# Expert units in another order: units of four experts beside single ones, and TensorE's order written by hand

## The chip, the cores and the metric

One core of one Trainium2 chip runs the whole program. A time is the device time of one execution in microseconds (us). Of the kernel before there are three timed runs (median 2342.96 us) and one execution under the hardware profiler, from which all rows below come.

## The reference, cut to what matters

Two model blocks run one after the other on 512 tokens of width 1024. The change lies in the last stage alone, the mixture of experts of the second block. Each token picks 6 of 64 experts and a shared one, and each expert is

```
def swiglu(x, wg, wu, wd):
    return (jax.nn.silu(x @ wg) * (x @ wu)) @ wd
# wg, wu: 1024 x 256 and wd: 256 x 1024 per expert
routed = sum over the 6 chosen experts of  w[token, e] * swiglu(h[token], wg[e], wu[e], wd[e])
y      = x + g2 * (routed + swiglu(h, shared));   out = rms_norm(y, final_g)
```

All is float32. The weights of the 64 experts are 201 MB and must all be read from HBM, whatever the tokens choose.

## The kernel before

The experts are ranked by how many tokens chose them, and `self.units` cuts the ranking into units of 128 token slots: 2 units of two experts at 64 slots whose experts are known ahead (T), 16 units of one expert at 128 slots (S), 14 units of two at 64 (P), 4 units of four at 32 (Q). The shared expert makes 4 more units of 128 tokens (H). `ORDER` (L2318) lists them in batches of two units of one kind. The loop of `moe` (L2189) walks through the units. For unit n:

- `start(n + 2)` orders the weights of the unit after next on SP's queue: three pieces of 1 MB per expert (gate and up for the first half of the width, for the second half, down) in the ring `er` of nine buffers (`NER`). A load waits only for a free buffer, so SP runs ahead of TensorE by up to nine pieces. For the first unit of a batch it also builds the one-hot matrix of the slots, and `slots` (products `pt`) turns it into token numbers and weights.
- `split_gu` (units S and H): ScalarE rounds each 128x512 weight tile to fp32r (`eh`, L2012), VectorE forms the rest (`el`, L2016); eight buffers each (`NEH`). A product is then three fast fp32r matmuls, eh·xh, el·xh, eh·xl. Units P and Q multiply the raw fp32 tiles: each expert uses 64 or 32 columns of the array, and those of the unit's two or four experts run side by side if they follow each other.
- `gate_up` (products `pg`, L2067), then silu on ScalarE and the multiplication on VectorE (`sg`), `hidden` (two transposes `pht`), `down` (products `py`, L2110), and the multiplication by g2 into `y`.
- `gather` (products `px`, L2048): half of the token rows of the next batch, picked with its one-hot matrix; 32 matmuls of 256 columns for each unit. `px` has two PSUM banks.
- `scatter`: GpSimd adds the `y` of the unit before to the output rows in HBM.

What stands in the loop is not the order in which engines work: the scheduler of the tile layer orders each engine's queue by its own estimates. At run time each engine works through its queue in order. `first`, `batch_slots(b)` and `c0 = 128 * (u % 2)` assume that both units of a batch have equally many experts. `finish` adds everything up and normalizes.

```
    NER = 9
    NEH = 8
    ONES, PAIRS, FOURS = 16, 28, 16
    ORDER = "T0 Q0 S0 P0 S1 P1 S2 P2 S3 H0 Q1 H1 S4 P4 S5 P5 S6 P6 S7 P3"
```

Of the kernel before, what the change touches and what calls it, by code (L numbers as in the profile page):

```python
# [7 lines left out]
F32 = mybir.dt.float32  # L8
F32R = mybir.dt.float32r
# [3 lines left out]
ALU = mybir.AluOpType  # L13
AX = mybir.AxisListType
# [23 lines left out]
class Builder:  # L38
# [1832 lines left out]
    def overflow_list(self):  # L1871

        nc = self.nc
        M = self.mx
        cnt = self.eid[:, 1]
        thr = M.tile([128, 4, 64], F32, name="thr")
        for a, b, c in self.CAPS:
            nc.gpsimd.memset(thr[:, 0, a:b], float(c))
        for j in range(1, 4):
            nc.gpsimd.tensor_scalar(thr[:, j], thr[:, 0], 128.0 * j, None, op0=ALU.add)  # L1880
        fcv = self.big("ovf").rearrange("p (a b c) -> p a b c", a=4, b=4)
        f, c, v = (fcv[:, i] for i in range(3))
        fl = lambda t: t.rearrange("p r e -> p (r e)")
        nc.vector.tensor_tensor(f, cnt[:, None, :].to_broadcast([128, 4, 64]), thr, op=ALU.is_gt)
        nc.vector.memset(v, 1.0)
        nc.vector.tensor_tensor_scan(fl(c), fl(v), fl(f), 0.0, op0=ALU.mult, op1=ALU.add)
        self.novf = self.mo.tile([128, 1], I32, name="novf")
        nc.vector.tensor_copy(self.novf, c[:, 3, 63:64])
        nc.vector.tensor_mul(c, c, f)
        nc.vector.tensor_scalar(c, c, -1.0, None, op0=ALU.add)  # L1890
        col = M.tile([128, 3], F32, name="ovcol", bufs=1)
        d = self.big("ovd")[:, :384].rearrange("p (a b) -> p a b", a=3)
        bc = lambda t: t[:, None, :].to_broadcast([128, 4, 64])
        for i, src in enumerate((bc(self.eid[:, 0]), bc(self.slot[:, 0:64]), thr)):
            nc.vector.scalar_tensor_tensor(v, c, self.pcol, src, op0=ALU.is_equal, op1=ALU.mult, accum_out=col[:, i:i + 1])
            nc.vector.tensor_scalar(d[:, i], self.ident, col[:, i:i + 1], None, op0=ALU.mult)
        pd = self.psg.tile([128, 3, 128], F32, name="pd", tag="px", bufs=2)
        nc.tensor.matmul(pd, self.ones, d, start=True, stop=True)
        self.ovexp = self.mo.tile([128, 2, 128], I32, name="ovexp")
        nc.vector.tensor_copy(self.ovexp, pd[:, 0:2])  # L1900
        self.ovoff = self.mo.tile([128, 128], F32, name="ovoff")
        nc.vector.tensor_copy(self.ovoff, pd[:, 2])
# [29 lines left out]
            self.places(oh, num)  # L1932
            self.finish([(self.ysplit(job["y"]), oh)])

    def onehot(self, pos, n, w):

        oh = self.xp.tile([128, NT, 256], F32R, name="oh", tag="oh", bufs=2)
        shape = [128, NT, n, w]
        self.nc.vector.tensor_tensor(oh[:, :, :n * w].rearrange("p t (n w) -> p t n w", n=n),
                                     pos[:, :, :, None].to_broadcast(shape),  # L1940
                                     self.slot1[:, None, None, :w].to_broadcast(shape), op=ALU.is_equal)
        return oh
# [30 lines left out]
            nc.vector.reduce_sum(num, sv[:, :, :u, 0], axis=AX.X)  # L1973
            nc.vector.tensor_scalar(num, num, 1024.0, None, op0=ALU.add)

    def batch_slots(self, b, num=None):

        rs = self.units[2 * b] + self.units[2 * b + 1]
        n, r = len(rs), slice(rs[0], rs[-1] + 1)
        u = slice(2 * b, 2 * b + 2)  # L1980
        oh = self.oh[b] = self.onehot(self.pos[:, :, r], n, 256 // n)
        self.slots(oh, self.vals[:, :, r], n, 256 // n, self.idx[:, r], self.wt[:, u], num)

    def raw(self, pool=None):
        return (pool or self.er).tile([128, 2048], F32, name="er", tag="er")
# [43 lines left out]
                for dn, raw in zip(job["dn"], job["raw"]):  # L2029
                    dn.append(self.wsplit(raw[2][:, k, h * 512:h * 512 + 512]))  # L2030

    def rows(self, rhs, h, whole, to=None):


        nc = self.nc
        n = rhs[0][1].shape[-1]
        x = [self.xp.tile([128, 4, 256], F32 if whole else F32R, name="xh", tag="xh", bufs=3) if to is None else
             to.rearrange("p (k n) -> p k n", k=4)]
        if not whole:
            x.append(self.my.tile([128, 4, 256], F32R, name="xl", tag="xl", bufs=2))  # L2040
        for q in range(2):
            for i in range(len(x)):
                px = self.psg.tile([128, 2, 256], F32, name="px", tag="px", bufs=2)
                for f in range(2):
                    k = 4 * h + 2 * q + f
                    ops = [(self.xt[t][p], oh) for t, oh in rhs for p in ((0, 1) if whole else (i,))]
# [3 lines left out]
                dst = x[i][:, 2 * q:2 * q + 2, :n]  # L2050
                if i == 0:
                    nc.scalar.copy(dst, px[:, :, :n])
                else:
                    nc.vector.tensor_copy(dst, px[:, :, :n])
        return x

    def gate_up_half(self, job, h):
# [3 lines left out]
        whole = job["whole"]  # L2061
        for k in range(4 * h, 4 * h + 4):
            x = [x[:, k % 4] for x in job["xs"][h]]
            for i, (x, w) in enumerate(((x[0], None),) if whole else ((x[0], 0), (x[0], 1), (x[1], 0))):
# [62 lines left out]
    def moe(self):  # L2127
# [8 lines left out]
        jobs = {}  # L2136
        nu = len(self.units)
        n = self.NSTAT // 2
        first = dict(T=0, S=n // 2, P=(n + self.ONES) // 2, Q=(n + self.ONES + self.PAIRS // 2) // 2)
        order = []  # L2140
        for b in self.ORDER.split():
            n = int(b[1:])
            if b[0] == "H":
                order += [f"s{2 * n}", f"s{2 * n + 1}"]
            else:
                order += [2 * (first[b[0]] + n), 2 * (first[b[0]] + n) + 1]

        def start(n):

# [14 lines left out]
            b = u // 2  # L2164
            if n == len(order) - 2:
                self.num = self.mj.tile([128, 2], F32, name="num")
            if b not in self.oh:
                self.batch_slots(b, self.num if n == len(order) - 2 else None)
            w = 128 // len(rs)
            es = []  # L2170
            for r in rs:
# [8 lines left out]
            jobs[u] = dict(whole=whole, down=whole, wt=self.wt[:, u:u + 1], c0=128 * (u % 2), raw=raw,  # L2180
                           parts=[(w * j, w) for j in range(len(rs))], caps=slots)
        def gather(n, h):

            if n >= len(order):
                return
# [2 lines left out]
                t = int(u[1])  # L2188
                rhs = [(t, self.idr[:, 128:384]), (t + 1, self.idr[:, 0:256])]  # L2189
            else:  # L2190
                rhs = [(t, self.oh[u // 2][:, t]) for t in range(NT)]
            xs[n] = xs.get(n, []) + [self.rows(rhs, h, jobs[u]["whole"])]
        xs = self.xs
        start(0)
        start(1)
        for n, u in enumerate(order):
            j = jobs[u]
            start(n + 2)
            j["xs"] = xs[n - n % 2]
# [10 lines left out]
                self.last_begin()  # L2210
            if "mem" not in j:
                self.gate_up(j)
                self.hidden(j)
            gather(n - n % 2 + 2, n % 2)
            if not j["down"]:
                self.split_down(j)
            if n and not late:
                for i in range(1, 4):
                    self.scatter(jobs[order[n - 1]], i)
            if "mem" not in j:  # L2220
                self.down(j)
            if n == 8:
                self.overflow_list()
                self.last_gain()

        nc.vector.tensor_scalar(self.fst[:, 0], j["sg"][:, :NT], 0.0, 1.0, op0=ALU.mult, op1=ALU.add)
        nc.scalar.activation(self.fst[:, 1], self.fst[:, 0], AF.Abs_reciprocal_sqrt)
# [5 lines left out]
    def last_gain(self):  # L2233

        nc = self.nc
        r = self.big("fgr")[:KD, :128]
        nc.sync.dma_start(r, self.a["final_g_2"].rearrange("(k p) -> k p", p=128))
# [5 lines left out]
    def last_begin(self):  # L2243
# [4 lines left out]
        for h in range(2):  # L2248
# [2 lines left out]
                nc.tensor.matmul(p[:, k], self.fgc[:, 4 * h + k:4 * h + k + 1].to_broadcast([128, 128]), self.ident, start=True, stop=True)  # L2251
            nc.scalar.copy(self.fgb[:, 512 * h:512 * h + 512], p)
        self.sum = [r[:, i * D:(i + 1) * D] for r in (self.raw() for _ in range(NT // 2)) for i in range(2)]
        for t in range(NT):
            nc.sync.dma_start(self.sum[t], self.racc[self.nsc % 2][t * 128:(t + 1) * 128])
# [13 lines left out]
    def finish(self, ys, more=None):  # L2269
# [4 lines left out]
        rows = [slice(t * 128, t * 128 + 128) for t in range(NT)]  # L2274
        if more:
            for t in range(NT):
                nc.sync.dma_start(more[t], self.racc[1 - self.nsc % 2][rows[t]])
        po = {}

        def mm(t, h):  # L2280
# [132 lines left out]
```

## Time and profile before

| what | value |
|---|---|
| timed runs, three | 2337.82, 2342.96, 2346.70 us |
| profiled execution, its own time | 2337.98 us |
| its span | 2335.9 us |
| TensorE busy (page) | 2220.7 us, 95% |
| VectorE, ScalarE, GpSimd busy | 59%, 43%, 18% |
| the stage of the experts | from about 1690 us to the end |
| its last `py` product | begins at 2303.70 us |
| mean transfer rate over the span | 178 GB/s |

In the page's strip of 40 slices the DMA engines are busy to 2 to 5 tenths before the stage and to 8 or 9 tenths in it, with 316 to 385 GB/s. TensorE's granted clock (PEclk) is full through nearly all of it. Busy time of TensorE counts from the start of a matmul to its modelled end, and matmuls overlap, so the distance from one start to the next tells more.

### The profile page before, as it was taken

How to read it: one execution, taken by the hardware profiler on the slowest of the kernel's cores; microseconds unless marked ns; L12 is line 12 of the kernel's file. 1: busy time of each engine (PE TensorE's matmuls, PEld its weight loads, DVE VectorE, ACT ScalarE, POOL GpSimd, SP SyncE). 2: the span in 40 equal slices, each digit the busy share in tenths (PEclk: the TensorE clock that was granted, in tenths of full speed). 3: DMA queues.
4: the chain of work that ended last, by engine and by line, in shares of the span. 5: the costliest groups of instructions: out<-in, count | busy, mean ns of one | idle time of the engine just before them, and what ended most of it. 6: DMA issues, size and time to landing. Idle time of an engine off the chain costs nothing. (4 is left out here: it accounts for less than half of the span.)

```text
span 2335.9 us, 31811 instructions
## 1 busy us (share of the span) xinstructions
PE 2220.7 (95%) x11699; PEld 1668.9 (71%) x11699; DVE 1381.9 (59%) x2439; ACT 1015.4 (43%) x1743; POOL 427.2 (18%) x354
## 2 busy tenths in 40 slices
PE   8999999999999999999889969999999999999995
PEld 6888888888777888888767656776655666466662
DVE  3658837854887686487557785774424555144444
ACT  4445515534786454354455525542313334133332
POOL 3023203310000322122302530002022011111110
PEclk9999999999999999999999978999999999999998
DMA  4235535435222443435045533326399989889894
GB/s 158 100 128 178 167 102 183 130 104 143 59 62 64 146 137 123 137 124 160 23 127 143 150 76 92 87 71 235 145 349 385 356 316 325 326 320 340 322 341 172
DMA packets 243809, 414.97 MB, mean 178 GB/s; under 512 B 35030, under 2 KB 135732, under 8 KB 243652
## 3 DMA queue, kind: packets, MB, share of 16 engines
q1 hardware_dynamic: 233444, 393.87, 48.7%
q0 software_dynamic: 5184, 13.90, 3.1%
q10 hardware_dynamic: 5024, 5.15, 1.0%
q8 instruction: 93, 1.52, 0.3%
q14 instruction: 64, 0.52, 0.1%
HBM read 378.93 MB, written 40.22 MB: 179 GB/s over the span
## 5 line engine op out<-in xcount | busy, mean ns | idle before, releaser
L93 DVE TENSOR_TENSOR wlo<-wraw,whi 128x2048 fp32r<-128x2048 f32 (+3 forms) x83 | 182.5, 2199 | 206.0 <-ACT whi L92 205.7
L135 PE MATMUL mm<-sgh,whi 128*128 128x512 f32 x768 | 300.8, 392 | 0.9 <-DVE hT L204 0.9
L136 PE MATMUL mm<-sgl,whi 128*128 128x512 f32 x768 | 299.2, 390 | 0.0
L137 PE MATMUL mm<-sgh,wlo 128*128 128x512 f32 x768 | 297.5, 389 | 0.0
L92 ACT CAST whi<-wraw 128x2048 fp32r<-128x2048 f32 (+3 forms) x83 | 146.1, 1761 | 210.6 <-PE mm L136 160.1
L746 POOL TENSOR_TENSOR adaacc<-adaacc,adaw 128x512 f32<-128x512 f32 x84 | 146.3, 1741 | 434.8 <-ACT adaw L745 431.7
L2067 PE MATMUL pg<-er,xh 128*64 128x512 f32 (+1 forms) x768 | 181.1, 599 | 4.7 <-DMA er<-in_exp_w_up 4.6
L2123 POOL DMA_INDIRECT racc<-y,idx x60 | 91.6, 1526 | 509.3 <-DVE y L2113 464.4
L135 PEld LDWEIGHTS mm<-sgh,whi 128*128 128x128 f32 x768 | 144.2, 188 | 30.9 <-issue 1.5
L137 PEld LDWEIGHTS mm<-sgh,wlo 128*128 128x128 f32 x768 | 144.2, 188 | 30.3 <-issue 0.2
L136 PEld LDWEIGHTS mm<-sgl,whi 128*128 128x128 f32 x768 | 144.2, 188 | 29.8 <-issue 0.5
L135 PE MATMUL mm<-ach,whi 128*128 128x512 f32 (+1 forms) x374 | 141.3, 378 | 0.0
L137 PE MATMUL mm<-ach,wlo 128*128 128x512 f32 (+1 forms) x374 | 140.9, 377 | 0.0
L136 PE MATMUL mm<-acl,whi 128*128 128x512 f32 (+1 forms) x374 | 140.8, 377 | 0.0
L2016 DVE TENSOR_TENSOR el<-er,eh 128x512 fp32r<-128x512 f32 x200 | 129.5, 685 | 18.2 <-ACT eh L2012 16.6
L2012 ACT CAST eh<-er 128x512 fp32r<-128x512 f32 x200 | 115.4, 620 | 50.8 <-PE pg L2067 32.3
L907 PE MATMUL mm<-nmh,zhi 128*128 128x512 f32 (+2 forms) x264 | 106.7, 405 | 10.5 <-DVE k L877 5.8
L2113 DVE TENSOR_TENSOR y<-py,g2b 128x512 f32<-128x512 f32 x76 | 52.3, 689 | 102.6 <-PE py L2110 102.4
L2067 PEld LDWEIGHTS pg<-er,xh 128*64 128x64 f32 (+1 forms) x768 | 48.3, 127 | 90.4 <-issue 85.6
L908 PE MATMUL mm<-nml,zhi 128*128 128x512 f32 (+2 forms) x264 | 103.9, 394 | 1.4 <-DVE nml L809 1.4
L909 PE MATMUL mm<-nmh,zlo 128*128 128x512 f32 (+2 forms) x264 | 103.0, 391 | 1.8 <-DVE zlo L899 1.8
L427 ACT ACTIVATE cv<-a,convw 128x512 f32<-128x512 f32 x88 | 70.5, 811 | 74.0 <-DVE a L425 74.0
(687 smaller groups left out, 5123.3 us busy)
## 6 DMA issues: line engine op xcount, KB each, us to landing
er<-in_exp_w_gate SPq DMA_DIRECT2D x128, 512.0 KB
er<-in_exp_w_up SPq DMA_DIRECT2D x128, 512.0 KB
er<-in_exp_w_down SPq DMA_DIRECT2D x64, 1024.0 KB
wraw<-in_f_w_in SPq DMA_DIRECT2D x32, 1024.0 KB
adaw<-in_ada_w SPq DMA_DIRECT2D x96, 256.0 KB
wraw<-in_f_w_down SPq DMA_DIRECT2D x16, 1024.0 KB
zraw<-in_w_in SPq DMA_DIRECT2D x30, 512.0 KB
wraw<-in_a_w_in SPq DMA_DIRECT2D x8, 1024.0 KB
```

Of the source, the lines that this page charges most:

```text
L92: nc.scalar.copy(hi[:, :n], raw[:, :n])
L93: nc.vector.tensor_sub(lo[:, :n], raw[:, :n], hi[:, :n])
L135: nc.tensor.matmul(to, wh[:, cols], xh, start=first, stop=False)
L136: nc.tensor.matmul(to, wh[:, cols], xl, start=False, stop=False)
L137: nc.tensor.matmul(to, wl[:, cols], xh, start=False, stop=last)
L746: nc.gpsimd.tensor_add(acc, acc, t)
L907: nc.tensor.matmul(ps[:n, part], hi[:, k, :n], xh, start=first and k == ks[0], stop=False)
L908: nc.tensor.matmul(ps[:n, part], hi[:, k, :n], xl, start=False, stop=False)
L909: nc.tensor.matmul(ps[:n, part], lo[:, k, :n], xh, start=False, stop=last and k == ks[-1])
L2012: nc.scalar.copy(hi, r)
L2016: nc.vector.tensor_sub(lo, r, hi)
L2067: nc.tensor.matmul(job["pg"][b:b + n], x[:, c:c + n], job["raw"][j][h][:, k % 4] if whole else job["gu"][j][k][w], start=k == 0 and i == 0 ...
```

## The change

`ORDER` becomes a list of letters, one per unit, in pairs, and each letter takes the next unit of its kind; the last two letters take the first units of theirs. Each Q now shares a batch with an S, so that the four Q stand in four batches instead of two. A mixed batch needs rows of two sorts from one gather: `rows` writes the exact rows of the Q half (rounded part plus rest, added on VectorE) and the rounded part and rest of the S half separately, in halves of 128 columns; `mixed_slots` does the slots of both. `gather` is cut in two: its first quarter-product stands between `gate_up` and `hidden`, its second between `hidden` and `down`, and `slots` move behind `gate_up`. TensorE's queue keeps this order as written (`manual_schedule`). The overflow list's product and the load of the last gain move one or two units.

```diff
-    def batch_slots(self, b, num=None):
+    def batch_onehot(self, us):
+        ra, rb = (self.units[u] for u in us)
+        if len(ra) == len(rb):
+            return self.onehot(self.pos[:, :, ra[0]:rb[-1] + 1], 2 * len(ra), 128 // len(ra))
+        oh = None
+        for i, r in enumerate((ra, rb)):
+            oh = self.onehot(self.pos[:, :, r[0]:r[-1] + 1], len(r), 128 // len(r), oh, 128 * i)
+        return oh
+    def batch_slots(self, us, oh, num=None):
...
+            self.mixed_slots(us, oh)
...
-    def rows(self, rhs, h, whole, to=None):
+    def rows(self, rhs, h, whole, to=None, x=None, qs=(0, 1)):
...
+            if mixed:
+                xs = x.pop().rearrange("p k (i n) -> p i k n", i=2)
+                x = [x[0][:, :, :128], xs[:, 0], xs[:, 1]]
+        part, full = (slice(0, 128), slice(128, 256))[::1 if whole == "split first" else -1]
-        for q in range(2):
-            for i in range(len(x)):
+        for q in qs:
+            for i in range(2 if mixed else len(x)):
...
+                if mixed and i == 0:
+                    nc.scalar.copy(dst[0], px[:, :, full])
+                    nc.scalar.copy(dst[1], px[:, :, part])
+                elif mixed:
+                    nc.vector.tensor_add(dst[0], px[:, :, full], dst[0])
+                    nc.vector.tensor_copy(dst[2], px[:, :, part])
...
-        for n, u in enumerate(order):
+        def unit(n, u):
...
             if "mem" not in j:
                 self.gate_up(j)
+            if n % 2 == 0:
+                slots(n + 2)
+            gather(n - n % 2 + 2, n % 2, 0)
+            if "mem" not in j:
                 self.hidden(j)
-            gather(n - n % 2 + 2, n % 2)
+            gather(n - n % 2 + 2, n % 2, 1)
             if not j["down"]:
                 self.split_down(j)
...
+        with self.tc.manual_schedule(engines={mybir.EngineType.PE}):
+            for n, u in enumerate(order):
+                unit(n, u)
...
-    ORDER = "T0 Q0 S0 P0 S1 P1 S2 P2 S3 H0 Q1 H1 S4 P4 S5 P5 S6 P6 S7 P3"
+    ORDER = "TT SQ SS PP SS SS PP SQ SS SS PP SQ HH PP PP HH PP SQ SS PP"
```

SP's queue at the first unit behind the two T units, before: the expert's number is read, then gate and up of the first half (a piece is a gate and an up load into one `er` buffer, or a down load); then the next expert's.

```order
L2172 TENSOR_LOAD eidi
L2002 ISA
L2002 DMA er<-in_exp_w_gate 128x1024
L2002 ISA
L2002 DMA er<-in_exp_w_up 128x1024
L2172 TENSOR_LOAD eidi
```

The same place in the changed kernel.

```order
L2242 TENSOR_LOAD eidi
L2044 ISA
L2044 DMA er<-in_exp_w_gate 128x1024
L2044 ISA
L2044 DMA er<-in_exp_w_up 128x1024
L2044 ISA
L2044 DMA er<-in_exp_w_gate 128x1024
L2044 ISA
L2044 DMA er<-in_exp_w_up 128x1024
L2047 ISA
L2047 DMA er<-in_exp_w_down 128x2x1024
L2242 TENSOR_LOAD eidi
```

Before, the 12 pieces of a unit of four stand here and 12 more of another such unit behind them. Now the three pieces of one expert come first, then the 12 of one unit of four, then 6 of two single units.

TensorE's queue where the second of the first two units of four begins, before (`py`: down products of the unit ahead of it, `px`: rows of a later batch, `pg`: gate and up).

```order
L2110 MATMUL py<-er,hh 32x512 x10
L2048 MATMUL px<-oh,xt3l 128x256
L2067 MATMUL pg<-er,xh 32x512
L2048 MATMUL px<-oh,xt0h 128x256
L2048 MATMUL px<-oh,xt1h 128x256
L2048 MATMUL px<-oh,xt2h 128x256
L2048 MATMUL px<-oh,xt3h 128x256
```

The first unit of four in the changed kernel, behind the last down products of its single partner.

```order
L2168 MATMUL py<-eh,hh 128x512
L2168 MATMUL py<-el,hh 128x512
L2168 MATMUL py<-eh,hl 128x512
L2125 MATMUL pg<-er,xh 32x512 x32
L2098 MATMUL px<-oh,xt0h 128x256
L2098 MATMUL px<-oh,xt1h 128x256
L2098 MATMUL px<-oh,xt2h 128x256
L2098 MATMUL px<-oh,xt3h 128x256
```

Before, one product of one expert stood alone between row products, and the others of its four came behind these; now all 32 products of the unit follow each other, and so do those of every unit of several experts but the last.

## Rows read from the trace of the kernel before

**Rows 1.** Stretches: length, busy us of PE, PEld, DVE, ACT, POOL; PEclk, DMA, GB/s.

```profile
1697.00:2307.00 610.00, 595.26 (x3300) 369.89 (x3297) 257.75 (x471) 185.66 (x357) 99.58 (x74) 1.00 0.93 337
1715.00:1765.00 50.00, 45.53 (x321) 26.54 (x319) 10.89 (x23) 9.08 (x18) 6.01 (x5) 1.00 1.03 403
2015.00:2065.00 50.00, 46.82 (x236) 24.09 (x232) 11.48 (x20) 10.24 (x21) 8.35 (x6) 1.00 0.89 347
2185.70:2248.40 62.70, 62.70 (x346) 40.39 (x345) 28.41 (x52) 22.06 (x42) 10.06 (x6) 1.00 0.96 353
```

**Rows 2.** TensorE, 1697 to 2307, forms: rows*columns, xcount, busy us, mean ns, idle before.

```profile
L2067 PE MATMUL pg<-er,xh 128*64 128x512 f32 x448 | 124.6, 600 | 0.0
...
L2067 PE MATMUL pg<-el,xh 128*128 128x512 f32 x160 | 64.8, 407 | 1.1 <-DVE el L2016 1.1
...
L2110 PE MATMUL py<-er,hh 128*64 128x512 f32 x224 | 52.3, 598 | 0.8 <-ACT hh L2092 0.8
...
L2067 PE MATMUL pg<-er,xh 128*32 128x512 f32 x256 | 41.9, 596 | 4.7 <-DMA er<-in_exp_w_up 4.6
...
L2110 PE MATMUL py<-er,hh 128*32 128x512 f32 x128 | 26.0, 600 | 0.0
...
L2110 PE MATMUL py<-el,hh 128*128 128x512 f32 x64 | 25.3, 395 | 0.0
...
L2110 PE MATMUL py<-er,hh 128*128 128x512 f32 x32 | 14.9, 598 | 0.0
```

**Rows 3.** The same stretches, instructions on the tile px alone.

```profile
1697.00:2307.00 610.00, 161.17 (x1123) 145.12 (x1123) 27.47 (x40) 43.48 (x75) 1.00 0.93 337
1715.00:1765.00 50.00, 17.85 (x128) 15.91 (x128) 2.75 (x4) 3.32 (x6) 1.00 1.03 403
```

**Rows 4.** TensorE lines, 1715 to 1765.

```profile
L2067 PE MATMUL pg<-er,xh 128*32 128x512 f32 x67 | 12.7, 596 | 2.5 <-DMA er<-in_exp_w_up 2.5
...
L2110 PE MATMUL py<-er,hh 128*32 128x512 f32 x64 | 11.1, 600 | 0.0
```

**Rows 5.** TensorE in order of time: start, us, what, count, [idle before].

```profile
1708.29 7.07 PE L2067 MATMUL pg<-er,xh 128*32 128x512 f32 x62
...
1715.52 0.28 PE L2048 MATMUL px<-oh,xt1h 128*128 128x256 f32 x1
...
1715.63 0.28 PE L2048 MATMUL px<-oh,xt2h 128*128 128x256 f32 x1
...
1729.13 1.04 PE L2067 MATMUL pg<-er,xh 128*32 128x512 f32 x2
...
1739.21 1.02 PE L2067 MATMUL pg<-er,xh 128*32 128x512 f32 x2 [1.96 <-DMA er<-in_exp_w_up]
```

**Rows 6.** TensorE in order of time, later.

```profile
2127.31 3.65 PE L2110 MATMUL py<-er,hh 128*64 128x512 f32 x16
...
2131.23 0.39 PE L2067 MATMUL pg<-eh,xl 128*128 128x512 f32 x1
...
2131.46 0.40 PE L2067 MATMUL pg<-eh,xh 128*128 128x512 f32 x1
```

**Rows 7.** Weight loads of TensorE in order of time.

```profile
1722.32 0.12 PEld L2110 LDWEIGHTS py<-er,hh 128*32 128x32 f32 x3 [0.31 <-issue]
...
1723.28 0.19 PEld L2048 LDWEIGHTS px<-oh,xt0h 128*128 128x128 f32 x1 [0.84 <-issue]
```

**Rows 8.** VectorE, forms, 1700 to 2300.

```profile
L2016 DVE TENSOR_TENSOR el<-er,eh 128x512 fp32r<-128x512 f32 x200 | 129.5, 685 | 18.2 <-ACT eh L2012 16.6 <-DMA er<-in_exp_w_gate 0.7 <-DMA er<-in_sh_w_up 0.3
...
L2082 DVE SCALAR_TENSOR_TENSOR sg<-pg,wt,sg 128x256 f32<-128x256 f32 x33 | 15.9, 482 | 73.7 <-ACT sg L2078 73.7
```

**Rows 9.** ScalarE, forms, 1700 to 2300.

```profile
L2012 ACT CAST eh<-er 128x512 fp32r<-128x512 f32 x200 | 115.4, 620 | 50.8 <-PE pg L2067 32.3 <-PE py L2110 7.6 <-DMA er<-in_exp_w_up 7.1
...
L2078 ACT ACTIVATE sg<-pg 128x256 f32<-128x256 f32 x37 | 14.1, 385 | 142.0 <-PE pg L2067 141.6
```

**Rows 10.** DMA queues: packets, MB, share of 16 engines over the span.

```profile
q0 software_dynamic: 5184, 13.90, 3.1%
```

More of the change, by code (lines that the diff above doesn't have):

```diff
@@ L1896, in overflow_list, with overflow_rows @@
             nc.vector.tensor_scalar(d[:, i], self.ident, col[:, i:i + 1], None, op0=ALU.mult)
+        self.ovd = d
+    def overflow_rows(self):
+        nc = self.nc
         pd = self.psg.tile([128, 3, 128], F32, name="pd", tag="px", bufs=2)
-        nc.tensor.matmul(pd, self.ones, d, start=True, stop=True)
+        nc.tensor.matmul(pd, self.ones, self.ovd, start=True, stop=True)
         self.ovexp = self.mo.tile([128, 2, 128], I32, name="ovexp")
@@ new lines, in batch_slots, with mixed_slots @@
+    def batch_slots(self, us, oh, num=None):
+        ra, rb = (self.units[u] for u in us)
+        if len(ra) == len(rb):
+            r = slice(ra[0], rb[-1] + 1)
+            self.slots(oh, self.vals[:, :, r], 2 * len(ra), 128 // len(ra), self.idx[:, r], self.wt[:, us[0]:us[0] + 2], num)
+        else:
+            self.mixed_slots(us, oh)
+    def mixed_slots(self, us, oh):
+        nc = self.nc
+        pt = self.psg.tile([128, 16, 4], F32, name="pt", tag="pt")
+        for i, u in enumerate(us):
+            rs = self.units[u]
+            n, w, c, r = len(rs), 128 // len(rs), 128 * i, slice(rs[0], rs[-1] + 1)
+            vals = self.vals[:, :, r]
+            for j in range(n):
+                for t in range(NT):
+                    nc.tensor.matmul(pt[:w, 4 * i + j], oh[:, t, c + j * w:c + (j + 1) * w], vals[:, t, j], start=t == 0, stop=t == NT - 1)
+            if n > 1:
+                for t in range(NT):
+                    nc.tensor.matmul(pt[:, 8:8 + n], oh[:, t, c:c + 128], vals[:, t], start=t == 0, stop=t == NT - 1)
+        for i, u in enumerate(us):
+            rs = self.units[u]
+            n, w, r = len(rs), 128 // len(rs), slice(rs[0], rs[-1] + 1)
+            nc.vector.tensor_scalar(self.idx[:w, r], pt[:w, 4 * i:4 * i + n, 0], 1024.0, None, op0=ALU.add)
+            sv = self.xp.tile([128, 4, 2], F32, name="svm", tag="svu", bufs=2)
+            if n == 1:
+                nc.vector.tensor_copy(sv[:, 0], pt[:, 4 * i, 1:3])
+                nc.vector.tensor_add(self.wt[:, u:u + 1], sv[:, 0, 0:1], sv[:, 0, 1:2])
+            else:
+                nc.vector.tensor_mul(sv[:, :n], pt[:, 8:8 + n, 1:3], self.own[:, n // 4, :n, None].to_broadcast([128, n, 2]))
+                nc.vector.reduce_sum(self.wt[:, u:u + 1], sv[:, :n], axis=AX.XY)
@@ L2045, in rows @@
                     k = 4 * h + 2 * q + f
-                    ops = [(self.xt[t][p], oh) for t, oh in rhs for p in ((0, 1) if whole else (i,))]
+                    ops = [(self.xt[t][p], oh) for t, oh in rhs for p in ((0, 1) if whole is True else (i,))]
                     for j, (xt, oh) in enumerate(ops):
@@ L2049, in rows @@
                                          start=j == 0, stop=j == len(ops) - 1)
-                dst = x[i][:, 2 * q:2 * q + 2, :n]
-                if i == 0:
-                    nc.scalar.copy(dst, px[:, :, :n])
+                dst = [d[:, 2 * q:2 * q + 2] for d in x]
+                if mixed and i == 0:
[4 more added lines that the diff above has]
+                    nc.vector.tensor_copy(dst[2], px[:, :, part])
+                elif i == 0:
+                    nc.scalar.copy(dst[0][:, :, :n], px[:, :, :n])
                 else:
-                    nc.vector.tensor_copy(dst, px[:, :, :n])
+                    nc.vector.tensor_copy(dst[1][:, :, :n], px[:, :, :n])
         return x
@@ L2063, in gate_up_half @@
             x = [x[:, k % 4] for x in job["xs"][h]]
+            if len(x) > 2:
+                x = x[:1] if whole else x[1:]
             for i, (x, w) in enumerate(((x[0], None),) if whole else ((x[0], 0), (x[0], 1), (x[1], 0))):
@@ L2138, in moe, with kind @@
         n = self.NSTAT // 2
[L2139 to L2144, printed above, removed]
-            else:
-                order += [2 * (first[b[0]] + n), 2 * (first[b[0]] + n) + 1]
+        kinds = dict(T=0, S=n, P=n + self.ONES, Q=n + self.ONES + self.PAIRS // 2)
+        last = self.ORDER[-2:]
+        tail = [kinds[last[0]], kinds[last[0]] + 1]
+        kinds[last[0]] += 2
+        order, sh = [], 0
+        for c in self.ORDER.replace(" ", "")[:-2]:
+            if c == "H":
+                order.append(f"s{sh}")
+                sh += 1
+            else:
+                order.append(kinds[c])
+                kinds[c] += 1
+        order += tail
+        assert sorted(order, key=str) == sorted([*range(nu), "s0", "s1", "s2", "s3"], key=str)
+        pairs = {n: order[n:n + 2] for n in range(0, len(order), 2)}
+        def kind(n):
+            if isinstance(order[n], str):
+                return None
+            wa, wb = (len(self.units[u]) > 1 for u in pairs[n])
+            return None if wa == wb else "whole first" if wa else "split first"
         def start(n):
@@ L2163, in start @@
                 return
[L2164 to L2168, printed above, removed]
+            if n % 2 == 0:
+                self.oh[n] = self.batch_onehot(pairs[n])
             w = 128 // len(rs)
@@ L2179, in start, with slots, gather @@
                     raw[j][i] = self.piece(e, i)
-            jobs[u] = dict(whole=whole, down=whole, wt=self.wt[:, u:u + 1], c0=128 * (u % 2), raw=raw,
+            jobs[u] = dict(whole=whole, down=whole, wt=self.wt[:, u:u + 1], c0=0 if kind(n - n % 2) else 128 * (n % 2), raw=raw,
                            parts=[(w * j, w) for j in range(len(rs))], caps=slots)
-        def gather(n, h):
+        def slots(n):
+            if n < len(order) and not isinstance(order[n], str):
+                if n == len(order) - 2:
+                    self.num = self.mj.tile([128, 2], F32, name="num")
+                self.batch_slots(pairs[n], self.oh[n], self.num if n == len(order) - 2 else None)
+        def gather(n, h, q):
             if n >= len(order):
@@ L2190, in gather @@
             else:
-                rhs = [(t, self.oh[u // 2][:, t]) for t in range(NT)]
-            xs[n] = xs.get(n, []) + [self.rows(rhs, h, jobs[u]["whole"])]
+                rhs = [(t, self.oh[n][:, t]) for t in range(NT)]
+            x = self.rows(rhs, h, kind(n) or jobs[u]["whole"], x=xs[n][h] if q else None, qs=(q,))
+            if q == 0:
+                xs[n] = xs.get(n, []) + [x]
         xs = self.xs
@@ L2218, in moe @@
                 for i in range(1, 4):
-                    self.scatter(jobs[order[n - 1]], i)
+                    self.scatter(jobs[order[n - 1]], i, self.lastacc if n == len(order) - 2 else None)
             if "mem" not in j:
@@ L2276, in finish @@
             for t in range(NT):
-                nc.sync.dma_start(more[t], self.racc[1 - self.nsc % 2][rows[t]])
+                nc.sync.dma_start(more[t], self.racc[self.lastacc][rows[t]])
         po = {}
```

33 lines of the change are left out of this document (18 added, 15 removed).

## The prediction

> **What bounds the kernel now.** I read the page's strip first (the change touches only the stage of the experts, from about 1690 us), then the stretches of that stage, then TensorE's lines and its order of time, then VectorE's and ScalarE's forms and the queues. The chain of waits ends in the last normalization and tells nothing of the stage.
>
> From 1697 to 2307 the stage looks bound twice: TensorE is busy 595 of 610 us and the DMA engines 0.93 of the time, at full granted clock (PEclk 1.00) [rows 1]. The busy time is too high, since matmuls overlap. So I count matmuls and multiply by the distance from start to start in a run that nothing breaks. A matmul on 64 columns takes 0.228 us (16 of them in 3.65) [rows 6], one on 32 columns 0.114 (62 in 7.07), a row product (px) 0.11 to 0.12 [rows 5], an fp32r product 0.23 [rows 6]. With the counts [rows 2, 3]:
> 672 on 64 columns: 153.2 us; 384 on 32: 43.8; 32 of the shared expert's down products at 14.9/32: 14.9; 672 fp32r (three forms each of 160 and 64, of which one stands): 154.6; 1123 px: 134.8; the other 417 of the 3300 at an estimated 0.09: 37.5. Sum 539 us. TensorE thus loses 71 us of the 610.
>
> The Trainium skill (Perfetto Trace Analysis, Identifying the Most-Contended Engine) says that matmul busy time is a poor measure and that the busy time of weight loads is a better one. Busy matmuls would leave 15 us to gain, busy weight loads (370 us) 240 us; the count above, from this trace, says 71.
>
> Where are they lost? From 1715 to 1765, where the first batch of two four-expert units (Q) runs, the counts give 67 x 0.114 + 64 x 0.114 + 128 x 0.12 + 62 others x 0.09 = 36 us of 50 [rows 1, 3, 4]: 14 lost. Weights come too late there: TensorE waits 1.96 us for an up weight at one place [rows 5], VectorE and ScalarE do little, and the DMA share is 1.03 [rows 1]. The same wait of the 32-column products is 4.6 us in the whole stage against 2.5 in this stretch [rows 2, 4], so the second Q batch (2015 to 2065) has nearly as much; I take 11 us for it, an estimate. The other 510 us lose 71 - 25 = 46, that is 4.5 us in 50. Above that ordinary loss the two Q batches cost 25 - 2 x 4.5 = 16 us.
>
> Much of the ordinary loss comes from broken runs. A run of two 32-column products alone takes 1.04 us where the count gives 0.23 [rows 5]; on 64 columns an unbroken group hides the second expert behind the first. In TensorE's order of time I count 62 runs of such gate and up products and 34 of down products, where 18 and 22 units need one each: 56 breaks, 19 of them leaving runs of two. A break costs about 0.5 us: the weight load behind a column run starts after 0.84 us of idle time against 0.31 within it [rows 7]. 56 x 0.5 = 28 us; at least the 19 short runs, 10 us, are certain.
>
> **The change part by part.**
>
> *The Q units spread.* A piece (1.05 MB) takes 2.6 us at 403 GB/s [rows 1], a scatter 3.1% x 2336 / 64 = 1.1 us of all DMA engines [rows 10]. By unit, transfers against TensorE (24 or 32 gate and up, 12 or 16 down, 32 px, small ones): S 9 us against 13; P (two experts) 18 against 15 to 16; Q 36 against 15 to 16. A batch QQ asks 72 us of transfers in 31 us of TensorE, and nine buffers hold 9 x 2.6 = 23 us of lead: it must wait, as seen. A batch SQ asks 45 against 29. Before it stand SS and PP: SS gives 26 - 18 = 8 us of lead, SS SS 16, PP takes 4 away, HH gives nearly all of its 23. So the lead is about 19 of 23 us at the second and third SQ, about 16 at the last, and 15 to 16 are spent in it. No wait inside, but 3 to 5 us of lead remain, and the unit behind it is a single one that needs its first two pieces (5.2 us) and a split (0.62 + 0.69 us) [rows 8, 9] before its first product: 2 to 3 us each time. The first SQ finds most of its 15 pieces loaded during the T units. I charge 9 us for all four. The ends: 0 (the lead holds), and 4 x 14.5 = 58 (no lead at all, 44.5 less 30). I take 9, near the low end, because the wait rows of the stage that name weights are small outside the Q batches (1.1 us on 160 fp32r products waiting for a split [rows 2]). Gain: 16 - 9 = 7 us.
>
> *TensorE's order by hand.* Every unit of several experts but the last now runs its gate and up and its down products unbroken. Returned: 10 to 28 us; I take 26, near the upper end, as the listing of the order shows no break left before the end.
>
> What is late next? In the fixed order TensorE waits where the scheduler would have put something else. Between gate_up and the transposes stand 16 px (1.9 us) and in half the units the slots; they must cover silu and the multiplication, 0.385 + 0.482 = 0.87 us [rows 8, 9]. Covered. Without cover it would cost 0.9 us in 38 units, 34 us. Two px banks serve four evictions per unit; where single follows single, the rest of the rows (xl, two buffers) is still held, one bank is stuck and the next gather waits for a copy of about 0.6 us: at most 1 us at two to six places. The eight split buffers keep VectorE's 12 splits x 0.685 = 8.2 us [rows 8] close behind TensorE in four single units in a row. I charge 5 us; ends -5 (the waits that the old order has there go too) and 34.
>
> *Mixed batches.* Same px count; four small evictions for two, on engines that are busy 186 and 258 of 610 us [rows 1]: beside TensorE's products, 0. If the cover were gone, two more copies of 0.3 us in 16 places, 5 us. Slots: 24 pt for SQ against 8 and 40 before: none. The moved overflow product and gain load: one matmul and one small load on SP past nine MB pieces that are queued anyway; 0. If that load held SP, 2 us once.
>
> **Sum.** 16 - 9 + 26 - 5 = 28 us off the profiled execution, 2337.98 us (span 2335.9, 2.1 around it), the lowest but one of four times: 2310 us. The tail behind the last product moves as a block. Against the median, 2342.96, it is 1.4% less; under 0.5%, 12 us, this kernel can't be told from no change.
>
> **The rivals.**
>
> *The transfers are the wall (15%).* If the lead at each SQ is only half of the buffers, 12 us, each batch runs short by 2.5 us and the unit behind it waits its full 6.5: 9 us, four times 36 instead of 9, and the gain is 0: 2338 us. For it: DMA share 0.93, so only 43 us are free in all. Against it: the free time lies in the stretches of S and H units, which now stand before Q.
> The Trainium skill (DMA: Bandwidth & Descriptors, Where 436 GB/s comes from) holds that transfers between HBM and SBUF are bound by HBM at about 358 GB/s per core. By that, an estimate from its figure, 183 pieces of 2.93 us and 72 us of scatters make 608 us, so nothing could be gained: 2338 us. The trace moves 403 GB/s for 50 us [rows 1], and the measurement decides; I leave the chance of this rival as it is.
>
> *Single units become the bound, slower (10%).* S units now stand four in a row twice. If the second half of a unit's splits can start only when down has freed the buffers, TensorE waits for four VectorE splits and one ScalarE split in each: 4 x 0.685 + 0.62 = 3.4 us [rows 8, 9], 16 times 54 us: 2364 us. It decides from 28 / 16 = 1.8 us per S unit. For it: ScalarE's and VectorE's order still comes from estimates, and one early wait there now holds TensorE. Against it: VectorE is busy 258 of 610 us, and in 2185 to 2248, with two S units, 28 of 63 [rows 1].
>
> *It goes better (20%).* No wait at SQ, all 28 us of breaks and 10 us of the other 18 ordinary: 16 + 28 + 10 = 54, cut to the 43 us that the DMA engines leave: 2295 us.
>
> **How the numbers follow.** My forecast has 55%, its own range 2297 to 2323. Faster by over 0.5% (under 2331): 55 + 20 + 3 of the transfer rival = 78%; within 0.5%: its other 12%; slower: 10%. The range takes in the better case and a little below it (transfer share over 1 in a saturated stretch hints at some 15 us more), and the transfer rival: 2280 to 2340.
>
> **What would show it.** Right: in the stretch of each SQ the waits for er are short; column products stand in 18 and 22 runs; no stretch of 50 us loses 14; DMA share of the stage about 0.97. Wrong: TensorE waiting on eh, el or sg in the S units (the slower rival), or on er in and behind each Q (the transfers). If the gain is right but Q still waits, the breaks cost more than 0.5 us.

## The result and the profile after

The changed kernel takes 2317.87 us (median of four, 2313.62 to 2325.68) against 2343.32 of the kernel before: ratio 0.9897, 95% interval 0.9863 to 0.9932. Timed again later: 0.9933, 0.9913 to 0.9953 (the run `again` below). By the medians it is faster by 15 to 25 us; the sum forecast 28 us off the profiled execution, which is 33 us off the median of before that was then known. By the intervals the gain is 0.5 to 1.4%, where 1.4% was forecast. The profiled execution took 2325.68 us, the slowest of its four; the time from the first down product (`pd`, the two T units) to the start of the last one (`py`), called the stage below, is 600.0 us in it, 602.3 in `again`, and 614.3 before.

The stretches, with the columns of [rows 1]; the first answers to its first row.

```profile
1697.00:2294.00 597.00, 569.10 (x3349) 370.33 (x3347) 263.79 (x511) 189.47 (x372) 96.36 (x74) 0.99 0.94 344
...
2036.00:2042.00 6.00, 4.93 (x27) 1.30 (x27) 0.00 (x0) 0.00 (x0) 0.00 (x0) 0.72 1.03 417
...
2131.00:2137.00 6.00, 5.52 (x16) 1.95 (x17) 0.00 (x0) 0.17 (x1) 0.00 (x0) 0.72 1.03 387
```

TensorE is now free for 28 us of the stage, not 15, and still done earlier: it does the same products in fewer, unbroken stretches and stands still between them. The two short stretches show a mean granted clock of 0.72, which [rows 1] had nowhere.

TensorE's forms, 1697 to 2307, columns as in [rows 2]:

```profile
L2125 PE MATMUL pg<-er,xh 128*64 128x512 f32 x448 | 102.8, 602 | 3.1 <-DMA er<-in_exp_w_up 3.1
...
L2125 PE MATMUL pg<-er,xh 128*32 128x512 f32 x256 | 34.8, 618 | 6.5 <-DMA er<-in_exp_w_up 6.5
...
L2168 PE MATMUL py<-er,hh 128*32 128x512 f32 x128 | 21.9, 597 | 7.9 <-DMA er<-in_exp_w_down 7.9
L2147 PE MATMUL pht<-ident,sg 128*128 128x128 f32 x76 | 14.9, 278 | 5.3 <-DVE sg L2140 5.3
```

With the same counts as in [rows 2] the busy time of the 64-column products falls from 124.6 to 102.8 us and that of the 32-column ones from 41.9 to 34.8: more products of different column groups now run side by side. What is new stands at the right: 17.5 us of waits for weights where there were 4.6, and 5.3 us for VectorE's product where the transposes waited 3.0 before.

TensorE in order of time in the first batch of a single unit and a unit of four (start, us, count, idle before):

```profile
1736.97 1.05 PE L2168 MATMUL py<-er,hh 128*32 128x512 f32 x4
1739.29 1.05 PE L2168 MATMUL py<-er,hh 128*32 128x512 f32 x2 [1.27 <-DMA er<-in_exp_w_down]
1741.85 3.62 PE L2168 MATMUL py<-er,hh 128*32 128x512 f32 x26 [1.51 <-DMA er<-in_exp_w_down]
1745.40 0.50 PE L2125 MATMUL pg<-eh,xh 128*128 128x512 f32 x1
1746.86 0.50 PE L2125 MATMUL pg<-el,xh 128*128 128x512 f32 x1 [0.96 <-DVE el L2058]
```

The gate and up weights were there in time, but down waits for its weights twice, and the single unit behind it for its split. The same shape, up to 2.0 us more between two products than the count gives, stands at the down products of all four units of four.

At the second and third of them gate and up weights come late too. The third:

```profile
2033.90 1.02 PE L2125 MATMUL pg<-er,xh 128*32 128x512 f32 x2 [2.33 <-DMA er<-in_exp_w_up]
2037.07 4.96 PE L2125 MATMUL pg<-er,xh 128*32 128x512 f32 x26 [2.15 <-DMA er<-in_exp_w_up]
```

Weights also come late at the last of the four two-expert units between the shared ones:

```profile
2127.68 1.49 PE L2125 MATMUL pg<-er,xh 128*64 128x512 f32 x6
2131.48 5.31 PE L2125 MATMUL pg<-er,xh 128*64 128x512 f32 x14 [2.31 <-DMA er<-in_exp_w_up]
```

Behind the wait 14 products take 5.31 us where 16 took 3.65 [rows 6]: that is the clock of 0.72 above, 3.4 us of it at 0.5.

To compare kernels I add up, for the stage, what each distance from one TensorE start to the next has beyond the count (0.215 us for 64 columns, 0.1075 for 32, 0.232 for fp32r, 0.118 for rows). "Broken" is this excess within column runs and at their ends, "half clock" what lies in stretches at granted clock 0.5, "weights" and "engines" are single excesses of 0.75 us or more at products of raw weights and at others. Stage and these sums are of the profiled execution alone, the ratios of all timed ones; for another trace of the same kernel compare `changed` and `again`.

| kernel | batches, order of TensorE | ratio to before | stage | broken | weights | engines | half clock |
|---|---|---|---|---|---|---|---|
| before | QQ, scheduler | 1 | 614.3 | 44.5 | 6.6 | 10.0 | 0 |
| like_batches | QQ, fixed | 0.9991 [0.9977, 1.0005] | 614.7 | 8.4 | 34.8 | 12.4 | 13.2 |
| sched_order | SQ, scheduler | 0.9987 [0.9973, 1.0001] | 614.7 | 41.1 | 0 | 16.0 | 1.9 |
| changed | SQ, fixed | 0.9897 [0.9863, 0.9932] | 600.0 | 11.9 | 22.9 | 9.6 | 5.2 |
| again | SQ, fixed | 0.9933 [0.9913, 0.9953] | 602.3 | 11.5 | 19.6 | 14.3 | 7.3 |
| sched_lead | SQ HH, scheduler | 1.0004 [0.9993, 1.0015] | 615.3 | 43.4 | 0 | 16.4 | 0 |
| lead_order | SQ HH, fixed | 0.9874 [0.9859, 0.9889] | 590.5 | 12.6 | 20.0 | 5.2 | 3.7 |
| sched_half | SQ half loads, scheduler | 0.9799 [0.9782, 0.9816] | 567.8 | 21.7 | 0 | 0 | 0 |
| half_fours | SQ half loads, fixed | 0.9817 [0.9792, 0.9841] | 579.8 | 3.1 | 3.3 | 17.7 | 8.7 |
| like_half | QQ half loads, fixed | 0.9780 [0.9763, 0.9796] | 570.9 | 2.6 | 0 | 17.1 | 4.7 |

### The profile page after: what moved, and what is told of

Its sections match the earlier page's. It is cut to its first block, busy times and chain, and to the rows that moved or that the text cites. A ratio compares the mean times of both kernels' runs of the same rounds, so it can differ in the third digit from the quotient of the medians.

```text
span 2323.6 us, 31933 instructions
## 1 busy us (share of the span) xinstructions
PE 2194.9 (94%) x11699; PEld 1669.0 (72%) x11699; DVE 1385.3 (60%) x2479; ACT 1020.4 (44%) x1759; POOL 425.0 (18%) x354
## 5 line engine op out<-in xcount | busy, mean ns | idle before, releaser
L2125 PE MATMUL pg<-er,xh 128*64 128x512 f32 (+1 forms) x768 | 152.2, 607 | 9.6 <-DMA er<-in_exp_w_up 9.6
L2058 DVE TENSOR_TENSOR el<-er,eh 128x512 fp32r<-128x512 f32 x200 | 125.9, 685 | 13.6 <-ACT eh L2054 13.2
L2136 ACT ACTIVATE sg<-pg 128x256 f32<-128x256 f32 x40 | 15.4, 384 | 214.8 <-PE pg L2125 214.5
```

Source lines behind the costliest of these rows:

```text
L2058: nc.vector.tensor_sub(lo, r, hi)
L2125: nc.tensor.matmul(job["pg"][b:b + n], x[:, c:c + n], job["raw"][j][h][:, k % 4] if whole else job["gu"][j][k][w], start=k == 0 and i == 0 ...
```

## The experiments

The theory from these traces: the fixed order of TensorE gives the time back that broken runs cost, and late weights and half clock take part of it. Its rivals: the spread of the fours does it; neither does it alone.

**The same kernel again.** 

> The changed kernel once more, as the measure for the others and for a second trace of it. Expected 2318 us, 313 to 326 as before it, 0.990 of the kernel before. If the stretches at half clock that follow a late weight load (three of 3.4 us, about 5 us in all) are a matter of the execution, the second trace shows another number of them; if they belong to the order, the same three.


Ratio 0.9933, median 2322.81 us. The second trace has four stretches of 3.4 us at half clock inside the stage, and only one of them (at 2274) stands where the first trace had one: they differ from execution to execution. Three follow single waits or pairs of waits of 1.3 to 2.3 us, the one at 2274 a wait of 2.0 us; other waits of 2.17 us (before 1827.36 and 2196.00) are followed by none. Two of the six waits for `sg` here (before 2009.77 and 2196.00, 4.8 us of the 14.3 under "engines") stand behind splits that wait for weights, so they too are late weights.

**The old batches in the fixed order.**

```diff
-    ORDER = "TT SQ SS PP SS SS PP SQ SS SS PP SQ HH PP PP HH PP SQ SS PP"
+    ORDER = "TT QQ SS PP SS PP SS PP SS HH QQ HH SS PP SS PP SS PP SS PP"
```

> The changed kernel with the batches of before (two units of four experts together, twice; ORDER is TT QQ SS PP SS PP SS PP SS HH QQ HH SS PP SS PP SS PP SS PP) but with TensorE's order fixed. Theory A, the fixed order alone brings the gain and the spreading nothing: 2318 us, within 6. As the prediction had it (spreading worth 7 us): 2325 us. Rival B: a fixed order can't put anything else into the waits of a batch of two fours; nine buffers hold 23 us of lead against 72 us of transfers in 31 us, so each of the two batches waits about 25 us and the fixed order loses there what it wins elsewhere: about 2340 to 2345 us, and then the spreading is what makes the fixed order pay.


2337.5 us, 0.9991: rival B. The broken runs are gone, yet all of it is lost again, nearly all in the two QQ batches, where all its long waits for weights stand; its waits:

```profile
PE pg L2125 <- DMA er<-in_exp_w_up: 18.6, 11, 3.7
PE pht L2147 <- DVE sg L2140: 8.3, 6, 2.0
PE py L2168 <- DMA er<-in_exp_w_down: 5.8, 6, 1.9
```

**The new batches in the scheduler's order.**

```diff
-        with self.tc.manual_schedule(engines={mybir.EngineType.PE}):
-            for n, u in enumerate(order):
-                unit(n, u)
+        for n, u in enumerate(order):
+            unit(n, u)
```

> The changed kernel with its new order of batches, but TensorE's order left to the scheduler again. Theory A, the gain is the unbroken column runs: 2318 + 26 - 5 = about 2339 us, and some 50 broken runs are back in the trace. If the spreading carried the gain: 2318 to 2325 us.


0.9987: the fixed order is needed. The broken runs are back: gate and up products stand in 76 runs (19 or 20 in the changed kernel, 67 before), if every other product counts as a break. The prediction's 62 for the kernel before leaves out breaks by slots and transposes. Spreading the fours alone brings nothing that can be told from zero.

**Half of the weights of the fours**, first in the fixed order:

```diff
-                    raw[j][i] = self.piece(e, i)
+                    raw[j][i] = raw[j - 2][i] if j >= 2 else self.piece(e, i)
```

> The changed kernel in which the third and fourth expert of each unit of four use the weights of its first and second, so that such a unit loads 6 pieces and not 12 (part of the weights is left out). If only the waits at these units cost (about 24 us of late weights and half clock in their batches by the trace, and some of the 6 us in the two-expert units behind the third): 2318 - 24 = 2294 us, down to 2290. If the transfers bind the whole stage, 24 pieces less are 24 x 2.6 = 62 us: about 2260 us. If the waits are hidden anyway: 2318 us.


2295.56 us, 0.9817, as the first case said: the waits cost, not the rate over the whole stage. But the waits for engines grew. The longest, in order of time for TensorE and then ScalarE:

```profile
2178.92 0.63 PE L2147 MATMUL pht<-ident,sg 128*128 128x128 f32 x2 [3.31 <-DVE sg L2140]
```

```profile
2175.32 2.18 ACT L2054 CAST eh<-er 128x512 fp32r<-128x512 f32 x4 [1.83 <-DMA er<-in_exp_w_up]
2177.40 0.37 ACT L2136 ACTIVATE sg<-pg 128x256 f32<-128x256 f32 x1
```

The silu stands behind four splits of the next unit in ScalarE's queue, and these wait for weights. So a part of what reads as a wait for VectorE is late weights too.

The same in the scheduler's order:


> The changed kernel with TensorE's order left to the scheduler and with units of four that load half of their weights (their third and fourth expert use those of the first and second, so part of the weights is left out). Against the run with half of these weights and the fixed order (0.982 of before) it prices the fixed order alone, where weights are on time. By the prediction's terms (26 us of broken runs, 5 us of new waits): 21 us slower, 0.991, about 2318 us. If the waits of the fixed order for VectorE (12.5 us there) and the half clock behind them eat half of it: 0.986. If unbroken runs bring nothing even with weights on time: 0.982.


0.9799, no slower than with the fixed order: the third case, and my price of the fixed order was wrong. The trace says why. The scheduler's runs are broken less here (51 of gate and up, by the same count) and TensorE waits for nothing longer than 0.5 us; the fixed order saves 21.7 - 3.1 = 18.6 us of broken runs and adds 3.3 + 17.7 + 8.7 = 29.7 us of waits and half clock. (The two profiled stages differ by 12 us, the ratios by 0.0018 or 4 us, within their intervals.) Against `sched_order` half of the loads take 46.9 us off the stage, although that run shows no long wait at products of raw weights: 19.4 of it are broken runs and 16.0 waits for other engines. The scheduler makes another order for it, and why both go was not tested.

And the fixed order with QQ batches:


> The changed kernel's fixed order of TensorE with the batches of before (two units of four together), and units of four that load half of their weights (part is left out, as above). If late weights are all that makes the fixed order fail with these batches (0.999 of before with all weights): the same as the spread batches with half of the weights, 0.982, within 0.002. If two units of four in a row cost something else as well (rows, copies, scatters): 0.987 or more.


0.9780, a little faster than the first case: with half of the loads two fours in a row cost nothing. Late weights were all that made these batches fail.

**Another order of batches.**

```diff
-    ORDER = "TT SQ SS PP SS SS PP SQ SS SS PP SQ HH PP PP HH PP SQ SS PP"
+    ORDER = "TT SQ HH PP HH PP SQ SS SS PP SQ SS PP SS PP SQ SS PP SS PP"
```

> The changed kernel with another order of the batches: both pairs of shared units stand behind a batch with a unit of four (ORDER is TT SQ HH PP HH PP SQ SS SS PP SQ SS PP SS PP SQ SS PP SS PP). Counted with nine buffers, 2.62 us a piece and the steps of each unit as the trace has them, TensorE waits 22 us for weights in place of 31 in the changed kernel's own order. If the lead of the ring decides: 2321 - 9 = 2312 us (0.9895 of before). If a unit of four waits anyway, because its 12 pieces are more than the ring, and the rest is nothing: 2321 us (0.993).


2311.73 us, 0.9874: the time of the first case. It is below the second timing of the changed kernel (0.9933), while the interval of the first timing (0.9863 to 0.9932) takes it in. The trace does not bear out the count behind it. TensorE still waits 20.0 us for weights, now all at the four units of four (19.0 there in the changed kernel, 16.6 in `again`), so they wait anyway, as the second case said:

```profile
PE py L2168 <- DMA er<-in_exp_w_down: 10.7, 8, 2.3
PE pg L2125 <- DMA er<-in_exp_w_up: 4.7, 3, 1.7
```

What is gone are the 3.9 us (2.9 in `again`) at the two-expert unit between the shared ones, 4.4 to 9.1 us of waits for other engines (4.3 of them at the first place where four single units follow each other; this order has one such place, the changed kernel two), and 1.5 to 3.6 us of half clock. These were not tested one by one. The DMA share of its stage is 0.96 and the rate 351 GB/s:

```profile
1697.00:2278.00 581.00, 559.10 (x3293) 363.81 (x3291) 257.36 (x495) 185.66 (x365) 102.70 (x73) 0.99 0.96 351
```

In the scheduler's order:


> The fastest order of batches so far (shared units behind the first two units of four) with TensorE's order left to the scheduler again. If the fixed order pays only where the transfers leave it little to wait for, and this order of batches does that: it loses what the fixed order gave, about 10 to 15 us against 0.987, so 0.992 to 0.994. If the order of batches does all by itself: 0.987. If the scheduler's order gains nothing from any order of batches (as with the spread ones): 0.999.


1.0004: nearest to the last case. Its trace shows TensorE waiting for no weights at all:

```profile
PE pht L2147 <- DVE sg L2140: 4.5, 3, 2.0
PE px L2098 <- ACT xh L2108: 4.0, 5, 1.0
PE pg L2125 <- DVE el L2058: 2.1, 3, 1.0
```

and SP's queue waiting for TensorE to free buffers, where in the changed kernel some 180 us of its 407 us of waits are for transfers ahead of its own (30 of 419 here). The two longest rows of each, first here, then in the changed kernel:

```profile
SPq L2044 <- PE pg L2125: 102.6, 23, 16.6
SPq L2047 <- PE pg L2125: 75.9, 19, 15.3
```

```profile
SPq L2044 <- DMA er<-in_exp_w_down: 67.0, 33, 3.9
SPq L2044 <- PE py L2168: 65.7, 9, 24.8
```

So the weights lie ready while TensorE works through broken runs. That the scheduler breaks them because it takes the transfers for slower than they are fits this, and that half the loads give fewer breaks; it was not tested by itself.

**Eight buffers.**

```diff
-    NER = 9
+    NER = 8
```

> The changed kernel with eight buffers for weights in place of nine. If the waits at the units of four come from the lead that the ring holds, each of the five places (four units of four, the last two of the units of two between the shared ones) and the end wait one piece, 2.6 us, longer: 2321 + 13 = 2334 us (0.9985). If the rate of the transfers alone sets them: 2321 us (0.993).


(With eight, one of the early down pieces of the first two units is another expert's, and one piece is loaded twice: 65 loads of down weights and not 64.) 2350.79 us, 1.0041 [1.0023, 1.006]: by the ratios 25 to 34 us more than the changed kernel, so more than the 13 expected, and surely not nothing. Its profiled execution is the fastest of the seven (2344.79 us), 19 to 21 us above those of the changed kernel, and 16 to 19 of these lie in the stage (618.6 us). There the waits for weights are 28.8 us (22.9 and 19.6 with nine buffers), those at the down products of the units of four 17.5 (11.3 and 12.7). Another 7.7 us are two waits of row products for copies (`xl`) that stand in ScalarE's queue behind splits which wait for weights; these had not been expected. At the first unit of four there are now three waits for down where nine buffers had two:

```profile
1737.79 1.04 PE L2168 MATMUL py<-er,hh 128*32 128x512 f32 x2
1740.20 1.04 PE L2168 MATMUL py<-er,hh 128*32 128x512 f32 x2 [1.36 <-DMA er<-in_exp_w_down]
1742.79 1.05 PE L2168 MATMUL py<-er,hh 128*32 128x512 f32 x2 [1.54 <-DMA er<-in_exp_w_down]
1745.36 3.19 PE L2168 MATMUL py<-er,hh 128*32 128x512 f32 x25 [1.52 <-DMA er<-in_exp_w_down]
```

**VectorE and ScalarE by hand** (the splits of the next unit are called between the steps of this one, at most two or four tiles at a time):

```diff
+            self.split_down(j, 2)
             gather(n - n % 2 + 2, n % 2, 0)
+            self.split_down(j, 1)
...
+            ahead(range(4))
...
-        with self.tc.manual_schedule(engines={mybir.EngineType.PE}):
+        with self.tc.manual_schedule(engines={mybir.EngineType.PE, mybir.EngineType.DVE, mybir.EngineType.Activation}):
```

> The changed kernel with the order of VectorE and ScalarE written by hand too: silu and the product stand ahead of the splits of the next unit, the splits of down behind them, those of the next unit's gate and up behind the row copies, and the copy of the last gain behind the silu of the last unit but one. Theory: in a fixed TensorE order the transposes wait for a product that stands behind splits in VectorE's queue (9.6 us in six places in the second trace), row products for copies (2.5 us), and half clock follows the long ones: 2321 - 12 to 15 = 2306 to 2309 us (0.987). Rival: VectorE is so full in single units (12 splits of 0.685 and 3.7 us else in 13 us) that its lateness only moves from the product to the splits: 2321 us (0.993), with waits for el where those for sg were.


0.9929 [0.9915, 0.9942], the same as without: the rival's result, but not for its reason. The waits for `sg` went (9.6 us in `again`, 1.0 here), but weights and row copies take most of that back, and `el` stayed where it was. All waits of TensorE are 29.1 us in `again` and 26.2 here, half clock 7.3 and 8.0:

```profile
PE pg L2131 <- DMA er<-in_exp_w_up: 12.9, 7, 3.5
PE py L2176 <- DMA er<-in_exp_w_down: 5.7, 4, 1.5
PE px L2103 <- DVE xl L2115: 2.4, 2, 2.3
PE px L2103 <- ACT xh L2113: 1.9, 3, 0.7
PE pg L2131 <- DVE el L2059: 1.2, 2, 1.0
PE py L2176 <- ACT hh L2158: 1.1, 2, 0.7
PE pht L2155 <- DVE sg L2148: 1.0, 1, 1.0
```

> Both: the order of batches of the kernel ahead of the last and VectorE and ScalarE by hand. If the two losses stand side by side they add: 2321 - 9 - 13 = 2299 us (0.983). If late weights fill the same gaps: 2306 us.


0.9895 [0.988, 0.991], not better than `lead_order`: a miss. The waits for `sg`, from which the gain was to come, are only 3.0 us in the trace of `lead_order`, and its waits for weights (15.4 us) stay nearly whole (14.4).

**The last gain later**, on `lead_order` (`last_begin` called behind `gate_up`):


> The order of batches that was fastest so far (0.987 of before), with the products and copies of the last gain moved behind the gate and up products of the last unit but one. In all traces of the fixed order ScalarE's silu of that unit stands behind these copies, which wait for a buffer of the weights, so the transposes wait 2.4 us and half clock follows for 3.4 us. If that is on the path to the end: 3 to 5 us less, 0.9855. If the tail then waits for the down weights instead (10 pieces of the last batch are on their way): 0.987.


0.9885 [0.9867, 0.9903], not to be told from 0.9874, with the wait of the last unit but one gone from the trace, a wait of 1.0 us at the last unit in its place, and the stage as long as before it (590.7 us). A few us at the tail are below what these runs can settle.

## Why the prediction was right, and where not

The time lies in the range, on the side that was forecast, but the stage of the traces gives back 14.3 us, half of the 28, and the terms are off both ways. From before to the changed kernel the table has broken -32.6, weights +16.3, half clock +5.2, engines -0.4, the rest -2.8. Its steps:

- *Unbroken runs, 26 us.* Right in mechanism and nearly in size: gate and up stand in 19 or 20 runs, down (without the shared expert's) in 18, and "broken" falls by 32.6 us from the kernel before and by 29.2 from `sched_order`. What it is worth is another matter: nothing clear of noise with QQ batches (0.9991), 12 to 21 us with SQ (0.9987 to 0.9933 or 0.9897), about 30 with the order of `lead_order` (1.0004 to 0.9874), and nothing with half loads. The step that failed is the one that put breaks and late weights side by side as two losses. While TensorE is broken up, the transfers catch up; made faster, it runs into them.
- *The Q units spread, 16 - 9 = 7 us.* Failed on both sides: a gain of 7 us was forecast, and the waits for weights grew by 16.3 us. The 16 us that the two QQ batches were to cost were put down to late weights. Counted as for the table, the two stretches [rows 1] of the kernel before lose about 8 and 10 us in broken runs and only about 3 each in waits for weights, so a good part of the 16 is the broken runs of the term above, counted twice. And "No wait inside" was wrong: of the 22.9 us that the changed kernel waits for weights, 3.9 stand at the two-expert unit between the shared ones and 19.0 inside the four Q units. I had charged 9, for the single unit behind each, which in fact waits once, 1.2 us for a split. 11.3 of the 19.0 stand at down products. Nine buffers can't hold a unit of 12 pieces: the last down pieces start only when its first gate and up pieces are used, and with eight buffers these waits are 17.5 us. The other 7.7 stand at gate and up products of the second and third Q, where I had counted the longest lead, 19 us; why it was shorter is not shown. Nor is 7 us a term of its own: spreading gives nothing in the scheduler's order (0.9987), 12 to 15 us of the stage in the fixed one (614.7 to 602.3 or 600.0). That a fixed order can't put other work into a wait fits this.
- *New waits in the fixed order, 5 us.* Waits for other engines are 9.6 us in one trace and 14.3 in the other, against 10.0 before and 16.0 in `sched_order`: that term is 0 to 4 us. The half clock behind long waits, 5.2 us (7.3 in `again`), I had not counted. The cover of `hidden` (16 row products) holds, except where silu or the product stands behind splits of the next unit, and at the last unit but one, where silu stands behind copies of the last gain that wait for a buffer.
- *Mixed batches, 0.* Nothing in the traces speaks against it.
- *The rivals.* The transfers are not the wall at 2338 us, though TensorE waits for them inside each Q, as that rival's sign has it: 344 GB/s and a share of 0.94 (0.97 was forecast), and `lead_order` gets more out of them. Single units don't bind: one takes 12.5 us where nothing waits, and at the two places where four single units follow each other row copies are late by 2.0 and 0.8 us and the product by 2.3 and 0.8, far from the 54 us of that rival. The better case, 2295 us, was reached by no order that was tried with all the weights.

From `sched_order` to the changed kernel in one line: broken -29.2, other small excess -7.4, engines -6.4, weights +22.9, half clock +3.3, counted work +2.1, together -14.7 us, as the stage shows (614.7 to 600.0). Most of the counted work is 16 row products that have no record in the trace of `sched_order`.

## What to carry to other kernels

Two losses that lie in the same stretch don't add: an engine that loses time by its own order hides transfers that would be late, so try each edit alone and both together before putting a price on either. A unit whose loads exceed the ring waited here whatever stood before it: 2.0 to 7.4 us for weights at each unit of four in the traces of the changed kernel and of `lead_order`. The order that puts work that loads little right behind two of these units was the fastest with all weights, but not by shorter waits in them.

## What had not been expected of the hardware

Around waits of TensorE of 2.15, 2.31 and 2.01 us (before 2037.07, 2131.48 and 2274.30 in the changed kernel; ahead of the first stood another of 2.33) the granted clock fell to 0.5, its level of 1.2 GHz, for 3.4 us each, and nowhere else in the stage; the kernel before had none there. A wait of 2.16 us (before 1829.59) was followed by none, and in `again` one stretch followed two waits of 1.3 and 1.5 us, so the length of a single wait does not settle it. In those stretches a group of column products side by side (four of 32 columns or two of 64) took 0.85 us in place of 0.43. In `like_batches` there are six such stretches, of 3.4 to 10.2 us, 13 us of excess in all. The Trainium skill (TensorE: Matmul & The Clock Gate, HAM oscillation) says that waits for transfers between bursts of matmuls bring the clock down; two of the three stretches here agree, and the third followed a wait for VectorE. A late weight can thus cost more than its wait, which no row of before could show.
